# First input projection of a two-layer diffusion backbone: which engine splits the first half's weights, and which weights are split a second time

## The chip, the cores and the metric

One core of one Trainium2 chip runs the whole program. The metric is the device time of one execution in microseconds (us); lower is better. The core has five engines with queues of their own that run in order: PE (matmul; PEld is its weight load), DVE (VectorE), ACT (ScalarE), POOL (GpSimd) and SP, which here only issues DMAs.

## The reference, cut to what matters

The change lies in the input projection of the first layer, `u = h @ w_in`: 2304 tokens (256 of context, 2048 latent) by 2816 columns with an inner size of 1024. Its columns go to the convolution branch (value and gate), to attention (q, k, v) and to the gate path z:

```python
def layer_ab(...):
    shift, scale, gate = adaln(c[:, None, :], w_ada, b_ada)
    h = rms_norm(x, norm_g) * (1 + scale) + shift
    u = h @ w_in
    a_val, a_gate = u[..., :A_WIDTH], u[..., A_WIDTH:AB_Q_OFF]
    q, k, v, z = ...                      # more columns of u
    y_a = conformer_conv(a_val, a_gate, conv_w, conv_b, ln_g, ln_b)   # depthwise, 31 taps
    y_b = blocked_attn(q, ...k, ...v)
    y = jnp.concatenate([y_a, y_b], axis=-1) * jax.nn.silu(z)
    x = x + gate * (y @ w_out)
```

All of it is float32, to float32 accuracy.

## The kernel before, in words

A float32 product is made of three matmuls on rounded halves. Each operand is split: ACT copies it to a rounded type (`hi`), and a second engine makes `lo = src - hi`. PE then adds hi·hi, hi·lo and lo·hi (`mm_channel`, lines 431 to 433, for outputs with channels on the partitions; `mm_token`, lines 440 to 442, for q, k and v). The second engine of the split is an argument: `split` (line 447) uses DVE unless told otherwise, `load_w` (line 399) uses POOL unless told otherwise.

The projection works in **two halves** of three token blocks of 384 (b = 0 to 2, then 3 to 5). In each half it goes through eleven **tasks**, each with its own 256 weight columns: g0, u0, g1, u1 (gate and value of the convolution), kv, q0, q1 and z0 to z3. A task of kind g, u or z makes six products of 24 matmuls; a task of kind kv or q makes nine, each followed by a chain of small steps in `qk`: ACT squares, DVE sums, POOL takes the power -0.5 (line 750), DVE scales (line 751), POOL multiplies by the rope tables (lines 755 and 759), DVE adds and splits (lines 763, 767, 770), PE transposes (line 779).

The weights of one task are two tiles (`kh` = 0, 1) in each of `whi` and `wlo`, whose pool `wp` holds four; so two tasks' weights fit, and a task's weights can be split only after the task before the last has released its tiles. In the first half `load_w` brings raw weights (`wraw`, two buffers) for the next task and splits them; `keep_w` writes the split halves to DRAM (`w_d`), and in the second half `kept_w` reads them back. g0 and u0 of the first half are special: they are loaded and split on DVE ahead of everything (`w_gu`, lines 618 to 645).

Beside this, DVE runs the depthwise convolution of the half as a background: `conv` yields one tap at a time (line 533, one instruction over 1151 or 1168 positions), and `advance` issues a number of taps before each product (3.2 or 3.6 for g, u and z, 1.1 after each q or k product). At the last z task of the first half, `prep_block` normalises, transposes (line 369), modulates (line 372, DVE) and splits (lines 380 and 381) the tokens of the second half.

The order on each engine is set by a scheduler with a timeline of its own, which places instructions by their data's availability on that timeline; taps are kept in program order. So an edit of an engine moves rows all around it.

Of the kernel before, what the change touches and what calls it, by code (L numbers as in the profile page):

```python
# [83 lines left out]
class Build:  # L84
# [365 lines left out]
    def ab_proj(self):  # L450
        nc, I, cp = self.nc, self.I, self.cp
        w = I["ab_w_in"][0]
# [3 lines left out]
        with ExitStack() as es:  # L456
# [4 lines left out]
            rp = self.pool(es, "rp", 2)  # L461
            wp = self.pool(es, "wp", 4)
# [24 lines left out]
            def small():  # L487
                rows = zp.tile([CONV, 512], F32, name="cwrows", tag="tz")
                nc.sync.dma_start(rows[:], I["ab_conv_w"][0])
                for c in range(4):  # L490
                    pt = pt_p.tile([P, 512], F32, name="cwt", tag="ptr")
                    nc.tensor.transpose(pt[:, :CONV], rows[:, c * P : (c + 1) * P], self.ident[:CONV, :CONV])
                    nc.vector.tensor_scalar(out=cw[:, c], in0=pt[:, :CONV], scalar1=0.5, scalar2=None, op0=ALU.mult)
                nc.sync.dma_start(cb[:], I["ab_conv_b"][0].rearrange("(c p) -> p c", p=P))
                for j, (nm, sgn) in enumerate((("ab_q_norm_g", -0.125), ("ab_k_norm_g", 1.0))):
                    g, gs = gain[:, 2 * j], gain[:, 2 * j + 1]
                    nc.sync.dma_start(g, I[nm][0:1, :].broadcast_to((P, 64)))
                    if sgn != 1.0:
                        nc.vector.tensor_scalar(out=g, in0=g, scalar1=sgn, scalar2=None, op0=ALU.mult)
                    nc.vector.tensor_copy(  # L500
                        gs.rearrange("p (i a) -> p i a", a=2), g.rearrange("p (i a) -> p i a", a=2)[:, :, ::-1]
                    )
# [13 lines left out]
            def advance(n):  # L516
                credit[0] = credit[0] + n if taps else 0.0
                while credit[0] >= 1 and taps:
                    f = taps.pop(0)
                    if next(f, None) is not None:  # L520
                        taps.insert(min(1, len(taps)), f)
                        credit[0] -= 1
# [56 lines left out]
            def convolve(j, us, half):  # L579
                for c, u in enumerate(us):  # L580
                    if half == 0:
                        nc.vector.tensor_copy(halo[:, 2 * j + c], u[:, 1151:1182])
                    taps.append(conv(u, 2 * j + c, half))
# [25 lines left out]
            ada, w_gu, hold = [], [], [[], []]  # L609
# [44 lines left out]
            for b in range(3):  # L654
# [8 lines left out]
                for c in range(2):  # L663
                    glu(0, c, b, us[c], sums[1, c, b])
                nxt[b] = hl[b]
            for i in range(2):
                self.keep_w(self.w_d[i], w_gu[i])
            small()
            ea.close()
            q3 = self.pool(er, "q3", 5, side="right")  # L670
            q2 = self.pool(er, "q2", 2, side="right")
            convolve(0, us, 0)
            ws_next = self.load_w(self.raws(rp), wp, w, 768)
            tasks = [("g", 0), ("u", 0), ("g", 1), ("u", 1), ("kv", 0), ("q", 0), ("q", 1), ("z", 0), ("z", 1), ("z", 2), ("z", 3)]
            col = {"g": 512, "u": 0, "kv": 1536, "q": 1024, "z": 1792}
            for half in range(2):
                blocks = range(3 * half, 3 * half + 3)
                for ti, (kind, j) in enumerate(tasks):
                    if half == 0 and ti < 2:
                        continue  # L680
                    ws = ws_next
                    if half == 0:
                        self.keep_w(self.w_d[ti], ws)
                    nk, nj = tasks[(ti + 1) % 11]
                    if half * 11 + ti < 10:
                        ws_next = self.load_w(self.raws(rp), wp, w, col[nk] + 256 * nj)
                    elif half * 11 + ti < 21:
                        ws_next = self.kept_w(wp, self.w_d[(ti + 1) % 11])
                    if kind in "guz":
                        for f in late:  # L690
                            next(f, None)
                        late.clear()
                        if half == 1 and (kind, j) == ("z", 0):
                            er.close()
                            self.load_kv()
                        if kind == "u":
                            us = pads(half, j)
                        order = [(c, b) for c in range(2) for b in blocks]
                        last = half == 0 and ti == len(tasks) - 1
                        if last or ti == 0:  # L700
                            order = [(c, b) for b in blocks for c in range(2)]
                        if half == 0 and 2 <= ti < 4:
                            for i in range(9):
                                rope(9 * ti - 18 + i)
                        for c, b in order:
                            advance(PZ[half] if kind == "z" else PG[half])
                            ps = mm_tile()
                            self.mm_channel(ps[:, :384], ws, nxt[b], c, slice(0, 384))
                            if kind == "g":
                                gate(j, c, b, ps)  # L710
                            elif kind == "u":
                                glu(j, c, b, us[c], ps)
                            else:
                                t = zp.tile([P, 384], F32, name="tz", tag="tz")
                                nc.scalar.activation(t[:], ps[:, :384], AF.Silu)
                                nc.scalar.dma_start(self.gz_d[2 * j + c, :, b * 384 : b * 384 + 384], t[:])
                            if last and c == 1:
                                prep_block(b + 3)
                        if kind == "u":
                            convolve(j, us, half)  # L720
                        continue
                    nh = 2 if kind == "kv" else 4
                    for b in blocks:
                        for i in range(3):
                            tt = 3 * b + i
                            ps = mm_tile()
                            self.mm_token(ps[:, :256], ws, nxt[b], slice(i * P, (i + 1) * P))
                            late.append(self.qk(qp, q2, q3, sp, pt_p, rope_d, ps, tt, kind, j, nh))
                            next(late[-1])
                            if len(late) > 3:  # L730
                                next(late.pop(0), None)
                            advance(PQ[half])
                for b in blocks:
                    del nxt[b]
# [1161 lines left out]
```

## Time and profile before

| what | us |
|---|---|
| median of 3 runs | 2914.79 |
| lowest, highest of them | 2907.32, 2920.73 |
| the profiled execution | 2907.36 |
| its span | 2905.6 |
| mean granted TensorE clock, share of full | 0.977 |

The profile is of one execution. Times in it run from its span's start; the projection takes about the first 685 us, and the first layer's attention follows. The rows on which the next section draws are shown ahead of it. Busy time is not time on the path: PE is busy almost everywhere, so what counts is where it stands idle or runs at the lower clock, and what ended that.

### The profile page before, as it was taken

The numbers are of one execution on the slowest core, as the hardware profiler recorded it, in microseconds if no ns is written. First come the engines' busy times: TensorE is split into PE (matmuls) and PEld (weight loads), VectorE is DVE, ScalarE is ACT, GpSimd is POOL, SyncE is SP. The second block draws the span as 40 slices with busy tenths as digits, with TensorE's granted clock in tenths as the row PEclk, the third lists the DMA queues.
The fourth block names the chain that finished last, engine by engine and source line by source line (L and its number), as shares of the span: only waits on it lengthen the run. The fifth ranks groups of instructions, "written<-read, shape, count | busy, mean of one in ns | idle before, by whom it ended". The sixth has DMA issues, their size and how long they took to land.

```text
span 2905.6 us, 40946 instructions
## 1 busy us (share of the span) xinstructions
PE 2752.1 (95%) x14481; PEld 2118.0 (73%) x14481; DVE 1825.2 (63%) x2867; ACT 1116.8 (38%) x2081; POOL 1416.4 (49%) x1151
## 2 busy tenths in 40 slices
PE   7998799999999999999999999999999997889898
PEld 5988799996444444444447788988898876788787
DVE  4798868898777878878977454101212246777563
ACT  3223120312445555555553223123222236677321
POOL 2568610711666787887885652222222214445342
PEclk9999899998999999999999999999999998999999
DMA  9546332474533433321216543333434269998862
GB/s 297 192 131 207 129 123 97 135 239 151 149 107 103 144 98 106 120 68 44 73 33 210 192 159 143 138 112 112 143 132 136 82 197 230 235 230 196 270 210 80
DMA packets 346808, 432.27 MB, mean 149 GB/s; under 512 B 55900, under 2 KB 260236, under 8 KB 341611
## 3 DMA queue, kind: packets, MB, share of 16 engines
q1 hardware_dynamic: 310891, 403.03, 46.2%
q10 hardware_dynamic: 35712, 26.62, 2.9%
q8 instruction: 114, 1.87, 0.3%
q14 instruction: 91, 0.75, 0.1%
HBM read 281.87 MB, written 152.84 MB: 150 GB/s over the span
## 4 chain that ended last, share of the span: by engine, by line
PE 62%; DMA 10%; DVE 3%; POOL 2%; issue 2%; ACT 1%; SPq 0%; POOLq 0%; ACTq 0%; DVEq 0%
PE av L922 9%; PE s L907 8%; PE mm L431 6%; PE mm L433 6%; PE mm L432 6%; PE m L884 6%; PE mo L1107 4%; PE mo L1108 4%; PE mo L1109 4%; DMA nv<-v_d 3%; DMA nk<-k 3%; PE mm L442 1%; PE mm L441 1%; PE mm L440 1%; DMA pat<-pat_d 1%
## 5 line engine op out<-in xcount | busy, mean ns | idle before, releaser
L886 DVE TENSOR_REDUCE ast<-m 128x1 f32<-128x512 f32 (+1 forms) x656 | 397.9, 626 | 145.9 <-PE m L884 143.8
L912 ACT ACTIVATE pr<-s 128x512 f32<-128x512 f32 x584 | 343.2, 595 | 311.7 <-PE s L907 269.6
L947 POOL TENSOR_TENSOR accp<-accp,pr 128x512 f32<-128x512 f32 x283 | 400.1, 1414 | 86.0 <-ACT pr L912 71.3
L447 POOL TENSOR_TENSOR wlo<-wraw,whi 128x1024 fp32r<-128x1024 f32 x64 | 202.4, 3169 | 380.3 <-ACT whi L446 380.2
L533 DVE SCALAR_TENSOR_TENSOR acc<-u,cw,acc 128x1151 f32<-128x1151 f32 (+1 forms) x240 | 353.0, 1526 | 0.0
L922 PE MATMUL av<-pr,vt 128*64 128x512 f32 x1168 | 315.7, 619 | 0.0
L433 PE MATMUL mm<-hi_ab,wlo 128*128 128x384 f32 x768 | 258.7, 338 | 16.8 <-POOL wlo L447 15.5
L432 PE MATMUL mm<-lo_ab,whi 128*128 128x384 f32 x768 | 259.8, 339 | 0.0
L431 PE MATMUL mm<-hi_ab,whi 128*128 128x384 f32 x768 | 256.2, 340 | 3.3 <-ACT hi_ab L380 1.9
L431 PE MATMUL mm<-hi_cd,whi 128*128 128x512 f32 x640 | 250.8, 392 | 1.1 <-ACT hi_cd L380 1.1
L432 PE MATMUL mm<-lo_cd,whi 128*128 128x512 f32 x640 | 250.1, 391 | 0.4 <-DVE lo_cd L381 0.4
L433 PE MATMUL mm<-hi_cd,wlo 128*128 128x512 f32 x640 | 246.7, 390 | 0.0
L947 DVE TENSOR_TENSOR accd<-accd,pr 128x512 f32<-128x512 f32 x165 | 169.2, 1026 | 1.3 <-DVE accd L947 0.5
L1664 DVE TENSOR_TENSOR nlo<-npt,nhi 128x512 fp32r<-128x512 f32 x192 | 123.6, 645 | 69.3 <-ACT nhi L1662 68.5
L884 PEld LDWEIGHTS m<-k1h,q 128*128 128x128 f32 x328 | 61.8, 188 | 133.8 <-DVE ast L886 79.8
L433 PEld LDWEIGHTS mm<-hi_ab,wlo 128*128 128x128 f32 x768 | 145.5, 190 | 17.8 <-POOL wlo L447 15.8
L884 PEld LDWEIGHTS m<-k0h,q 128*128 128x128 f32 x328 | 63.5, 196 | 125.2 <-DVE ast L886 82.1
L1626 POOL TENSOR_SCALAR npr<-npr,nst 128x640 f32<-128x640 f32 (+1 forms) x128 | 108.0, 857 | 89.5 <-DVE nst L1625 64.1
L372 DVE TENSOR_SCALAR ht<-ptr,scale,shift 128x384 f32<-128x384 f32 (+2 forms) x96 | 61.2, 671 | 141.1 <-PE ptr L369 140.5
L431 PEld LDWEIGHTS mm<-hi_ab,whi 128*128 128x128 f32 x768 | 144.9, 190 | 5.3 <-ACT hi_ab L380 2.9
L432 PEld LDWEIGHTS mm<-lo_ab,whi 128*128 128x128 f32 x768 | 145.4, 189 | 0.9 <-issue 0.8
L431 PEld LDWEIGHTS mm<-hi_cd,whi 128*128 128x128 f32 x640 | 120.4, 188 | 26.1 <-ACT hi_cd L380 1.6
(321 smaller groups left out, 6931.4 us busy)
## 6 DMA issues: line engine op xcount, KB each, us to landing
wraw<-in_cd_w_in_dram SPq DMA_DIRECT2D x46, 512.0 KB, 3.8
pat_d<-big SPq DMA_DIRECT2D x72, 256.0 KB, 4.0
nk<-k SPq DMA_DIRECT2D x32, 576.0 KB, 12.7
pat<-pat_d SPq DMA_DIRECT2D x24, 768.0 KB, 6.0
nv<-v_d SPq DMA_DIRECT2D x128, 128.0 KB, 7.3
adaraw<-in_ab_w_ada_dram SPq DMA_DIRECT2D x24, 512.0 KB, 8.2
adaraw<-in_cd_w_ada_dram SPq DMA_DIRECT2D x24, 512.0 KB, 3.7
w_d<-whi SPq DMA_DIRECT2D x22, 512.0 KB, 2.8
```

Of the source, the lines that this page charges most:

```text
L431: nc.tensor.matmul(ps, a, hh[:, k, cols], start=k == 0, stop=False)
L432: nc.tensor.matmul(ps, a, hl[:, k, cols], start=False, stop=False)
L433: nc.tensor.matmul(ps, b, hh[:, k, cols], start=False, stop=k == KT - 1)
L447: (eng or nc.vector).tensor_tensor(out=lo, in0=src, in1=hi.bitcast(F32), op=ALU.subtract)
L533: ins = nc.vector.scalar_tensor_tensor(out=acc[:, :n], in0=u[:, tap : tap + n], scalar=cw[:, ch, tap : tap + 1], in1=acc[:, :n], op0=ALU.m ...
L884: nc.tensor.matmul(ps[:, :n], lhs, kt[hp // 2][0][:, a : a + n], start=True, stop=True)
L886: nc.vector.tensor_reduce(out=s["st"][:, qt, col : col + 1], in_=ps[:, :n], axis=AX.X, op=ALU.min)
L907: nc.tensor.matmul(ps[:], kt[hp // 2][key][:, k * P : k * P + P], s[x][:].rearrange("p j n -> p (j n)"), start=key == 0, stop=key == 1,)
L912: nc.scalar.activation(pr[:], ps[:], AF.Exp, scale=-1.0)
L922: nc.tensor.matmul(s["av"][x * 64 : x * 64 + 64], vt[:, k - 1 + x, kv * 64 : kv * 64 + 64], s["pr"][k - 1 + x][:], start=k == 1, stop=k == ...
L947: eng.tensor_tensor(out=s[name][:], in0=first_in[:], in1=s["pr"][k][:], op=ALU.add)
L1664: return lambda: nc.vector.tensor_tensor(out=lo[:, :o], in0=pt[:, :o], in1=hi[:, :o].bitcast(F32), op=ALU.subtract)
```

## The change

The first-half weights from g1 to z3 (nine tasks, 18 splits) are split by DVE in place of POOL. The weights of g0 and u0 are no longer written to DRAM; when the second half needs them they are loaded raw and split once more, by DVE (4 splits). The reads of kept weights remain for the other nine tasks of the second half.

```diff
@@ ab_proj
                 nxt[b] = hl[b]
-            for i in range(2):
-                self.keep_w(self.w_d[i], w_gu[i])
             small()
...
             convolve(0, us, 0)
-            ws_next = self.load_w(self.raws(rp), wp, w, 768)
+            ws_next = self.load_w(self.raws(rp), wp, w, 768, eng=nc.vector)
...
-                    if half * 11 + ti < 10:
-                        ws_next = self.load_w(self.raws(rp), wp, w, col[nk] + 256 * nj)
+                    if half * 11 + ti < 12:
+                        ws_next = self.load_w(self.raws(rp), wp, w, col[nk] + 256 * nj, eng=nc.vector)
                     elif half * 11 + ti < 21:
-                        ws_next = self.kept_w(wp, self.w_d[(ti + 1) % 11])
+                        ws_next = self.kept_w(wp, self.w_d[ti + 1])
```

In the order that the scheduler makes, three places matter. Line numbers of the changed kernel behind its line 665 are two lower than before: its line 761 is 763 before, 765 is 767.

**DVE in the z tasks, before.** From the last step of the last q product (`hl`) to the first block of the second half; `acc` are convolution taps, `ht` is line 372, `lo_ab` line 381.

```order
L763 TENSOR_TENSOR t_3055<-t_3055,qsq 128x256
L767 TENSOR_TENSOR hl<-t_3055,hl 128x4x64
L533 SCALAR_TENSOR_TENSOR acc<-u,cw,acc 128x1151 x47
L372 TENSOR_SCALAR ht<-ptr,scale_234,shift_233 128x384 x2
L533 SCALAR_TENSOR_TENSOR acc<-u,cw,acc 128x1151
L372 TENSOR_SCALAR ht<-ptr,scale_234,shift_233 128x384
```

The same place in the changed kernel; the three pairs of `wlo` are the splits for z2, for z3 and for the second g0.

```order
L765 TENSOR_TENSOR hl<-t_3047,hl 128x4x64
L533 SCALAR_TENSOR_TENSOR acc<-u,cw,acc 128x1151 x2
L336 TENSOR_SCALAR st<-st 128x1
L533 SCALAR_TENSOR_TENSOR acc<-u,cw,acc 128x1151 x6
L447 TENSOR_TENSOR wlo<-wraw,whi 128x1024
L533 SCALAR_TENSOR_TENSOR acc<-u,cw,acc 128x1151 x2
L447 TENSOR_TENSOR wlo<-wraw,whi 128x1024
L533 SCALAR_TENSOR_TENSOR acc<-u,cw,acc 128x1151 x12
L447 TENSOR_TENSOR wlo<-wraw,whi 128x1024
L533 SCALAR_TENSOR_TENSOR acc<-u,cw,acc 128x1151
L447 TENSOR_TENSOR wlo<-wraw,whi 128x1024
L533 SCALAR_TENSOR_TENSOR acc<-u,cw,acc 128x1151 x15
```

After these stand the pair for g0 with one tap between, four taps, and then the first `ht`. So 47 taps have become 43 taps and six splits.

**DVE at the end of the first second-half block, before.** These are the last rows of block 3 and the first `u` of the second half.

```order
L372 TENSOR_SCALAR ht<-ptr,scale_234,shift_233 128x384 x2
L533 SCALAR_TENSOR_TENSOR acc<-u,cw,acc 128x1151 x2
L381 TENSOR_TENSOR lo_ab_3812<-ht,hi_ab_3811 128x384 x2
L564 COPY u<-halo 128x31
L336 TENSOR_SCALAR st<-st 128x1
L575 SCALAR_TENSOR_TENSOR u<-tg,mm 128x384
```

The same rows in the changed kernel.

```order
L372 TENSOR_SCALAR ht<-ptr,scale_234,shift_233 128x384 x2
L447 TENSOR_TENSOR wlo<-wraw,whi 128x1024
L533 SCALAR_TENSOR_TENSOR acc<-u,cw,acc 128x1151
L447 TENSOR_TENSOR wlo<-wraw,whi 128x1024
L533 SCALAR_TENSOR_TENSOR acc<-u,cw,acc 128x1151
L381 TENSOR_TENSOR lo_ab_3808<-ht,hi_ab_3807 128x384 x2
L533 SCALAR_TENSOR_TENSOR acc<-u,cw,acc 128x1151 x4
```

The pair of splits for the second u0 now stands ahead of the last two `lo_ab` of block 3. Its `whi` copies stand likewise on ACT, and they write tiles that z3 uses to its end.

**POOL among the last q products and in the z tasks, before.** `qst` is line 750, `t` and `qsq` are lines 755 and 759.

```order
L755 TENSOR_TENSOR t_2946<-qraw,tab 128x256
L759 TENSOR_TENSOR qsq<-qraw,tab 128x256
L755 TENSOR_TENSOR t_3000<-qraw,tab 128x256
L759 TENSOR_TENSOR qsq<-qraw,tab 128x256
L750 TENSOR_TENSOR qst<-qst,mhalf 128x4
L340 TENSOR_SCALAR xt<-xt,st 128x1024
L339 TENSOR_TENSOR st<-st,mhalf 128x1
L340 TENSOR_SCALAR xt<-xt,st 128x1024
L755 TENSOR_TENSOR t_3055<-qraw,tab 128x256
L759 TENSOR_TENSOR qsq<-qraw,tab 128x256
L447 TENSOR_TENSOR wlo<-wraw,whi 128x1024 x4
```

The same place in the changed kernel.

```order
L753 TENSOR_TENSOR t_2992<-qraw,tab 128x256
L757 TENSOR_TENSOR qsq<-qraw,tab 128x256
L753 TENSOR_TENSOR t_3047<-qraw,tab 128x256
L757 TENSOR_TENSOR qsq<-qraw,tab 128x256
L339 TENSOR_TENSOR st<-st,mhalf 128x1
L340 TENSOR_SCALAR xt<-xt,st 128x1024
L565 MEMSET u 128x15
```

POOL has no split left; under the z tasks it holds only the scaling of one token tile (lines 339 and 340), which belongs to block 4.

## Rows read from the trace of the kernel before

**Rows 1.** The view of windows, one for each stretch of the projection: kv, q0 and q1 of the first half; the same of the second half; z0 to z2; the wait ahead of z3; z3; second g0. Columns: stretch, its length, then PE, PEld, DVE, ACT and POOL busy us (instructions), granted clock, DMA share, GB/s.

```profile
152.10:258.00 105.90, 92.47 (x717) 90.69 (x717) 94.82 (x154) 31.93 (x83) 77.59 (x74) 0.92 0.47 150
490.60:579.20 88.60, 85.36 (x715) 84.08 (x713) 73.87 (x139) 25.64 (x74) 61.08 (x67) 1.00 0.43 137
258.00:336.60 78.60, 77.49 (x457) 76.75 (x457) 73.57 (x66) 23.04 (x42) 55.21 (x23) 1.00 0.56 190
336.60:352.60 16.00, 0.49 (x3) 0.17 (x1) 13.76 (x11) 0.49 (x1) 16.00 (x2) 0.60 0.03 12
352.60:382.20 29.60, 29.59 (x169) 29.41 (x170) 19.08 (x23) 5.28 (x11) 2.29 (x1) 0.93 0.47 165
382.20:415.70 33.50, 31.24 (x192) 29.60 (x191) 21.11 (x43) 15.23 (x30) 8.23 (x12) 1.00 0.37 145
```

**Rows 2.** The view of waits, PE, 0 to 700 us. Columns: us in total, times, longest.

```profile
PE mm L433 <- POOL wlo L447: 15.5, 1, 15.5
```

**Rows 3.** The instructions on the tile `wlo`, 0 to 700 us: count, shortest/median/longest in ns, first and last start in us.

```profile
L447 POOL TENSOR_TENSOR wlo<-wraw,whi x18: 2370/2918/41862, 93.1 to 352.5; 128x1024 fp32r<-128x1024 f32 x18
L447 DVE TENSOR_TENSOR wlo<-wraw,whi x2: 1217/1222/1226, 22.2 to 24.8; 128x1024 fp32r<-128x1024 f32 x2
```

**Rows 4.** The timeline of POOL, 286 to 360 us: start, length, what, count, idle time before it and what ended that.

```profile
288.26 2.93 POOL L447 TENSOR_TENSOR wlo<-wraw,whi 128x1024 fp32r<-128x1024 f32 x1 [7.10 <-ACT whi L446]
292.68 3.31 POOL L447 TENSOR_TENSOR wlo<-wraw,whi 128x1024 fp32r<-128x1024 f32 x1 [1.49 <-ACT whi L446]
310.70 44.20 POOL L447 TENSOR_TENSOR wlo<-wraw,whi 128x1024 fp32r<-128x1024 f32 x2 [14.70 <-ACT whi L446]
```

**Rows 5.** The timeline of DVE, 283 to 400 us.

```profile
283.54 66.82 DVE L533 SCALAR_TENSOR_TENSOR acc<-u,cw,acc 128x1151 f32<-128x1151 f32 x47
363.12 1.26 DVE L372 TENSOR_SCALAR ht<-ptr,scale,shift 128x384 f32<-128x384 f32 x2 [12.76 <-PE ptr L369]
...
383.90 1.02 DVE L381 TENSOR_TENSOR lo_ab<-ht,hi_ab 128x384 fp32r<-128x384 f32 x2
```

**Rows 6.** The timeline of PE around the wait ahead of z3.

```profile
336.75 0.34 PE L432 MATMUL mm<-lo_ab,whi 128*128 128x384 f32 x1
352.61 0.69 PE L433 MATMUL mm<-hi_ab,wlo 128*128 128x384 f32 x1 [15.53 <-POOL wlo L447]
```

**Rows 7.** The view of windows right behind that wait, columns as in Rows 1.

```profile
352.60:356.70 4.10, 4.09 (x13) 4.09 (x14) 0.00 (x0) 0.00 (x0) 2.29 (x1) 0.50 0.56 221
356.80:361.00 4.20, 4.20 (x26) 4.20 (x25) 0.00 (x0) 0.49 (x1) 0.00 (x0) 1.00 0.88 298
```

**Rows 8.** The timeline of ACT in z2: the evictions of its last two products.

```profile
332.61 0.49 ACT L715 ACTIVATE tz<-mm 128x384 f32<-128x384 f32 x1 [3.67 <-PE mm L433]
...
336.77 0.49 ACT L715 ACTIVATE tz<-mm 128x384 f32<-128x384 f32 x1 [3.67 <-PE mm L433]
```

**Rows 9.** The view of groups by line, DVE, of four stretches in this order: 104 to 283 us, 300 to 351, 490.6 to 579.2 and 600 to 680. Columns: count, busy us, mean ns of one, idle time before.

```profile
L533 DVE SCALAR_TENSOR_TENSOR acc<-u,cw,acc 128x1151 f32<-128x1151 f32 x63 | 102.6, 1663 | 0.0
...
L533 DVE SCALAR_TENSOR_TENSOR acc<-u,cw,acc 128x1151 f32<-128x1151 f32 x38 | 50.6, 1417 | 0.0
...
L533 DVE SCALAR_TENSOR_TENSOR acc<-u,cw,acc 128x1168 f32<-128x1168 f32 x26 | 41.1, 1592 | 0.0
...
L533 DVE SCALAR_TENSOR_TENSOR acc<-u,cw,acc 128x1168 f32<-128x1168 f32 x58 | 78.3, 1429 | 0.0
```

**Rows 10.** The timelines of DVE and POOL, 125 to 134 us.

```profile
124.78 9.68 DVE L533 SCALAR_TENSOR_TENSOR acc<-u,cw,acc 128x1151 f32<-128x1151 f32 x4
...
126.27 6.98 POOL L447 TENSOR_TENSOR wlo<-wraw,whi 128x1024 fp32r<-128x1024 f32 x2 [6.61 <-ACT whi L446]
```

**Rows 11.** The view of waits, PE: first four rows kv to q1 of the first half (152.1 to 258 us), last two the same of the second half (490.6 to 579.2).

```profile
PE ptr L779 <- ACT hl L769: 5.0, 1, 5.0
PE ptr L779 <- DVE hl L767: 3.9, 3, 1.6
PE mm L440 <- DVE qraw L751: 3.1, 3, 1.5
PE mm L440 <- DVE u L575: 1.3, 1, 1.3
...
PE mm L440 <- DVE qraw L751: 2.9, 4, 0.8
PE ptr L779 <- DVE hl L767: 0.3, 1, 0.3
```

**Rows 12.** The view of windows, stretches of lower clock between kv and q1, columns as in Rows 1.

```profile
172.40:179.30 6.90, 6.51 (x31) 6.51 (x32) 6.40 (x14) 2.19 (x8) 4.74 (x6) 0.51 0.30 86
227.00:230.50 3.50, 2.90 (x13) 2.90 (x14) 3.38 (x3) 1.20 (x3) 3.50 (x3) 0.51 1.00 350
240.60:247.50 6.90, 4.99 (x24) 4.83 (x25) 5.73 (x12) 2.55 (x6) 4.31 (x6) 0.51 0.37 105
```

**Rows 13.** Groups by line, ACT, 85 to 420 us, and the page, part 6 (DMA issues: count, KB each, median us to landing).

```profile
L446 ACT ACTIVATE whi<-wraw 128x1024 fp32r<-128x1024 f32 x18 | 19.1, 1060 | 33.4 <-PE mm L432 29.6 <-DMA wraw<-in_ab_w_in_dram 2.4 <-PE mm L433 1.5
...
wraw<-in_cd_w_in_dram SPq DMA_DIRECT2D x46, 512.0 KB, 3.8
...
w_d<-whi SPq DMA_DIRECT2D x22, 512.0 KB, 2.8
```

## The prediction

> **What bounds the kernel now.** I read the windows of the projection first. PE is busy nearly all of each stretch but one: ahead of z3 there are 16.0 us with three PE instructions [rows 1]. The view of waits names one wait of 15.5 us, PE's first matmul with `wlo` of z3 on POOL's split [rows 2], and PE's timeline shows the same 15.53 us between 336.75 and 352.61 [rows 6]. The reader is to see next what that split is: POOL's 18 weight splits of the first half take 2.37 us at least and 2.92 in the median, and one takes 41.86 [rows 3]. It starts at 310.70, as soon as its `whi` is there, and its successor ends the pair's 44.20 us [rows 4]. DVE tells the rest: from 283.54 it runs 47 taps without a pause for 66.82 us, to 350.36 [rows 5], and the long split ends some 2 us after, about what a split takes by itself. So POOL stood behind DVE's taps for as long as these came without a gap. The other two splits under this run took 2.93 and 3.31 [rows 4].
>
> The second place is kv to q1: 105.9 us in the first half and 88.6 in the second for the same matmuls, at a mean granted clock of 0.92 against 1.00 [rows 1]. There PE waits 5.0 + 3.9 + 3.1 + 1.3 = 13.3 us for the chain of small steps and a late eviction, against 3.2 us in the second half [rows 11], and 17.3 us run at half clock, the level of 1.2 GHz, with 14.4 us of PE work [rows 12].
>
> **Part 1: the long split goes.** In the changed order z3's splits stand on DVE, behind 22 taps and two other splits from the end of the last q product. A tap without POOL beside it takes 50.6 / 38 = 1.33 us of DVE's time [rows 9], a DVE split 1.22 [rows 3]. With the 47-tap run's start at 283.54 as the anchor, z3's first split starts at about 283.5 + 22 × 1.33 + 2 × 1.22 = 315 and the second ends near 319. Its `whi` needs the end of z1, near 312, so DVE does not wait there either. PE asks for it at 336.75 [rows 6]: 18 us of slack. The 15.5 us go. Behind the wait PE runs 13 matmuls in 4.1 us at 0.50 and then 26 in 4.2 at 1.00 [rows 7], so the lower clock that follows costs 4.1 / 2 = 2.05 us, and goes too. Together **-17.6 us**.
>
> What is late next is block 3's preparation, which DVE does behind its taps. Before, DVE had finished the run at 350.36 and then sat idle 12.76 us for PE [rows 5]. Without the wait, PE reaches z3 at 336.75, needs 8.3 us for two products (4.16 each, the distance of two evictions [rows 8]), transposes three column groups, and after 33 further matmuls (33 / 24 × 4.16 = 5.7 us) wants their buffers back: about 352. DVE gets to the first `ht` after 43 taps and six splits, 283.5 + 43 × 1.33 + 6 × 1.22 = 348. So this holds with 4 us to spare if DVE reaches the anchor no later than now.
>
> **Part 2: does DVE reach the anchor as early?** Up to the first `ht`, 20 splits of 1.22 us are new on DVE. The two of g1 fall where DVE has little to do, ahead of the taps; 18 remain, 22.0 us. But POOL's splits were not free to DVE. Four taps with two POOL splits beside them took 9.68 us [rows 10], where 4 × 1.33 = 5.3: 2.2 us for each split, nearly twice what DVE needs to do it itself. Likewise the 47 taps: 66.82 - 62.5 = 4.3 us for the two splits under them [rows 5]. From 104 to 283 us 63 taps took 102.6 where 83.8 were enough [rows 9]: 18.8 us too many. Part of this is POOL's work for q, which stays: in the second half, without splits, 26 taps between kv and q1 took 41.1 where, at 78.3 / 58 = 1.35, 35.1 were enough [rows 9], so 6.0. The relief is 18.8 - 6.0 + 4.3 = 17.1, at the most 16 × 2.2 = 35 and at the least the 8.7 us of the four splits seen singly. I take 17.1, since it rests on 63 taps. Net, DVE's load grows by 5 us (13 at the most, -13 at the least) over 180 us in which it is nearly full, and loses four taps (5.3 us) ahead of the first `ht`: **0 on the path**, with 4 us of slack.
>
> By a rule of the Trainium skill (the page SBUF — State Buffer, section "Who interferes with whom") the port that VectorE and GpSimd share is held for one whole instruction by whoever starts first, also against a VectorE instruction with two SBUF inputs; taken by itself it would let a split wait one tap, as 2.93 and 3.31 us do, and not some thirty, as 41.86 does. It would make the long split an accident with another cause.
>
> **Part 3: kv to q1.** Six splits leave POOL and six come to DVE. The ends are 0 and the full distance to the second half, 105.9 - 88.6 = 17.3. Each first wait of 5.0 and 1.3 us stands at the start of kv, where DVE is behind with taps; there the relief is larger than the added splits, two POOL splits costing 4.4 and two DVE splits 2.4. The later waits, 7 us, hang on DVE's chain, which gets no lighter. I take the first kind, less what DVE cannot make up: **-5 us**.
>
> **Part 4: second u0.** DVE's pair of splits for u0 stands ahead of the last two `lo` of block 3, and needs the tiles that z3 frees at its end. With z3 from 336.75 and 29.6 - 2.05 us long [rows 1, 7], it ends near 364.3. DVE, from 348, has eight `ht`, eight `lo` (1.26 and 1.02 us a pair [rows 5]) and ten taps before the last `lo` of block 3: 5.0 + 4.1 + 13.3, and the pair of splits 2.4, which gives 373. The second g0 needs that `lo` 18 matmuls after z3's end, 3.1 us, at 367.4. ACT's copies, 1.06 us each [rows 13], are ready by 366 and are no bound. New wait: 3 to 6 us, less what DVE gains in part 3, and up to half of a stretch like 172.4 to 179.3 at half clock [rows 12], 3.3 us. Between 0 and 9, I take **+5 us**.
>
> **Part 5: queues.** SP issues eight writes less near the start and, for g0 and u0, four raw loads in place of eight reads (3.8 and 2.8 us to landing [rows 13]); no PE wait on these reads is among those that end now, so 0. ACT has four more copies, 4.2 us, in stretches where it is busy less than a third [rows 1]: 0. Behind block 3 the order is that of before and nothing else moves.
>
> **Sum.** -17.6 - 5 + 5 = -17.6 us on the profiled execution, 2907.4 to 2889.8. That execution lies at the bottom of the four known (2907.3, 2907.4, 2914.8, 2920.7, middle 2911.1). From the middle the sum gives 2893.5; I write **2894 us**.
>
> **The rivals.** *The stall is handed on to DVE.* If the relief of part 2 is at its lower end, DVE's load grows by 13 us, the first `ht` comes near 361 and PE, at 352, waits 9 us, with 2 to 3 us of half clock behind it; the last `lo` moves back as much, so part 4 costs 9, and part 3 gives nothing: -17.6 + 11.5 + 9 = +3, 2914. For it: DVE runs 66.82 us without a gap [rows 5], and from kv to q1 is busy 94.8 of 105.9 us [rows 1]. Against it: 2.2 us for each POOL split under taps [rows 10].
>
> *The long split is an accident.* One of 18 is long [rows 3]; if most executions do not have it, part 1 falls away: -5 + 5, 2911. This is also what the rule of the Trainium skill cited in part 2 (SBUF — State Buffer, "Who interferes with whom") gives. Against it: a run without the stall would be some 17 us shorter, and of the three timed ones none is below the profiled.
>
> *Slower: DVE's queue stops at splits whose tiles PE has not yet freed.* The pairs for q1, z0, z1, g0 and u0 each need the end of a task on PE, and PSUM evictions for PE stand behind them on DVE. It decides once DVE comes to them ahead of PE by more than PE's free PSUM tiles cover. The nearest price is the longest wait of PE for that chain, 5.0 us, with 3.3 of half clock behind it [rows 11, 12]; five times 8.3 is 41.5, against 17.6 gained: +24, 2935. Against it: DVE is the one that is behind in most of the half.
>
> **Chances.** Forecast 0.58, handed on 0.22, accident 0.12, slower 0.08. About 0.5% (14.6 us) is what a measurement of this kernel can tell from no change. The forecast's gain, 17.6 with terms that can each be off by 5, exceeds that in nine of ten of its cases: faster 0.52; same takes the rest of it and the next two rivals, 0.40; slower 0.08. The range runs from the forecast with 12 us more in part 3, or with no wait in part 4, 2878, to the handed-on stall, 2914.
>
> **What would show it.** In the profile after: no POOL work on `wlo`, no PE wait ahead of z3, z3 starting its first 48 matmuls right behind z2 (part 1); taps of 1.33 us in the z tasks and fewer long ones before (part 2); kv to q1 nearer 100 than 106 us (part 3); a PE wait for `lo` of block 3 in the second g0, a few us long (part 4). I am wrong if PE waits in z3 for `ht` by more than 5 us, if a POOL step of the q chain is starved under taps, or if the first half's tasks from g1 to z2 get longer.

## The result, and the profile after

| | median us | lowest, highest | executions | ratio to before, 95% interval |
|---|---|---|---|---|
| before | 2916.62 | 2907.32, 2920.73 | 4 | |
| changed | 2892.37 | 2889.40, 2895.14 | 4 | 0.993 [0.9904, 0.9955] |
| changed, in a later series (before there: 2910.20, 25 executions) | 2890.28 | 2881.68, 2906.29 | 8 | 0.9936 [0.9913, 0.996] |

The kernel is faster by 0.7%, some 20 us; 2894 was forecast. The profiled execution took 2895.14 us, its span is 2893.3 at a mean granted clock of 0.978. In the changed kernel a line behind 665 has a number two lower than before.

The windows of the same stages as in [rows 1]: kv to q1, z0 to z2, z3, second g0; columns as there.

```profile
154.20:252.30 98.10, 89.05 (x715) 87.84 (x713) 86.08 (x154) 31.06 (x81) 64.67 (x68) 0.95 0.50 159
252.40:329.80 77.40, 77.35 (x457) 77.14 (x457) 72.65 (x73) 25.23 (x44) 20.83 (x18) 1.00 0.65 222
329.80:357.70 27.90, 27.90 (x172) 27.77 (x172) 27.90 (x31) 7.90 (x14) 0.00 (x0) 1.00 0.32 105
357.70:396.70 39.00, 33.16 (x189) 31.55 (x188) 30.74 (x50) 16.28 (x31) 7.37 (x12) 0.91 0.21 72
```

z3 with the wait ahead of it took 16.0 + 29.6 = 45.6 us; it takes 27.9, all of it PE work. kv to q1 is 7.8 us shorter: PE's idle time there goes from 105.90 - 92.47 = 13.4 to 9.0 us, and its busy time falls by 3.4 us as the granted clock rises from 0.92 to 0.95. The second g0 is 5.5 us longer. From the view of waits, PE, 0 to 700 us, the row `PE mm L433 <- POOL wlo L447` of [rows 2] is gone. Of 154.2 to 252.3 us, kv to q1, these three rows are all that it has, in place of the four of [rows 11].

```profile
PE mm L440 <- DVE qraw L749: 4.0, 3, 2.4
PE mm L440 <- ACT vv L771: 2.9, 2, 2.4
PE ptr L777 <- DVE hl L765: 2.1, 2, 1.6
```

The splits, all on DVE (as [rows 3]):

```profile
L447 DVE TENSOR_TENSOR wlo<-wraw,whi x24: 1206/1216/1758, 21.9 to 360.6; 128x1024 fp32r<-128x1024 f32 x24
```

The group of the taps from 104 to 283 us (as the first of [rows 9]):

```profile
L533 DVE SCALAR_TENSOR_TENSOR acc<-u,cw,acc 128x1151 f32<-128x1151 f32 x69 | 98.5, 1456 | 0.0
```

The timeline of DVE from the last split for the second g0 to the last taps of the first half (as [rows 5]):

```profile
333.57 1.22 DVE L447 TENSOR_TENSOR wlo<-wraw,whi 128x1024 fp32r<-128x1024 f32 x1
334.71 5.40 DVE L533 SCALAR_TENSOR_TENSOR acc<-u,cw,acc 128x1151 f32<-128x1151 f32 x4
340.02 1.85 DVE L372 TENSOR_SCALAR ht<-ptr,scale,shift 128x384 f32<-128x384 f32 x3
...
363.08 1.01 DVE L381 TENSOR_TENSOR lo_ab<-ht,hi_ab 128x384 fp32r<-128x384 f32 x2
364.02 5.39 DVE L533 SCALAR_TENSOR_TENSOR acc<-u,cw,acc 128x1151 f32<-128x1151 f32 x4
```

No split takes over 1.8 us, 69 taps now fit into 98.5 us where 63 took 102.6, and DVE is at the first `ht` at 340.0, ten us behind z3's start at 329.8, early enough that PE does not wait there.

**The new gap in the second g0.** It does not hang on block 3's `lo`, which DVE has done at 364.1. Its chain, followed from PE backwards, begins with PE's timeline:

```profile
371.37 0.34 PE L433 MATMUL mm<-hi_ab,wlo 128*128 128x384 f32 x1
376.58 0.90 PE L369 MATMUL ptr<-ident,xt 128*128 128x128 f32 x3 [4.88 <-POOL xt L340]
```

POOL's, with the tile that PE waited for:

```profile
374.75 0.56 POOL L339 TENSOR_TENSOR st<-st,mhalf 128x1 f32<-128x1 f32 x1 [5.17 <-DVE st L336]
375.41 1.12 POOL L340 TENSOR_SCALAR xt<-xt,st 128x1024 f32<-128x1024 f32 x1
```

DVE's step ahead of it, which waited for ACT's sum of squares:

```profile
374.51 0.15 DVE L336 TENSOR_SCALAR st<-st 128x1 f32<-128x1 f32 x1 [2.14 <-ACT jk L335]
```

SP's, with the load of that tile:

```profile
368.96 0.44 SPq L325 DMA_DIRECT2D xt<-in_x_dram  x1
```

And the window right behind the gap, columns as above:

```profile
376.60:381.80 5.20, 4.85 (x18) 4.16 (x19) 4.85 (x9) 3.18 (x8) 4.99 (x6) 0.50 0.01 3
```

PE stands still for 4.88 us and then runs 5.2 us at 0.50, the level of 1.2 GHz. It waits for POOL's normalised token tile, the third of block 4; that waits for the sum of squares, and that for the load issued at 368.96. The tile is taken from the pool `up`, which also holds the convolution's input `u`, and the load is issued while DVE ends the last four taps (364.02 to 369.41), which free their `u` tiles. In SP's queue it stands right behind two writes of `acc`, which wait for the same taps. In the kernel before, this load went out 3.4 us behind z3's end and PE waited 1.0 us for the tile; here it went out 11.3 us behind.

From the first matmul to the end of the projection the terms are: start of kv +2.1, kv to q1 -7.8, z0 to z2 -1.2, z3 -17.7, second g0 +5.5, the rest +1.8 us; its last matmul ends at 667.4 in place of 684.7 us, 17.3 earlier. The whole profiled execution is only 12.2 us shorter; experiment 5 says why.

### The profile page after: what moved, and what is told of

It is laid out like the page before. It is cut to its first block, busy times and chain, and to the rows that moved or that the text cites. A ratio compares the mean times of both kernels' runs of the same rounds, so it can differ in the third digit from the quotient of the medians.

```text
span 2893.3 us, 40920 instructions
## 1 busy us (share of the span) xinstructions
PE 2755.2 (95%) x14481; PEld 2118.0 (73%) x14481; DVE 1821.2 (63%) x2889; ACT 1120.5 (39%) x2085; POOL 1329.2 (46%) x1133
## 4 chain that ended last, share of the span: by engine, by line
PE 61%; DMA 11%; DVE 3%; POOL 2%; issue 2%; ACT 1%; SPq 0%; POOLq 0%; ACTq 0%; DVEq 0%
PE av L920 8%; PE s L905 8%; PE mm L433 6%; PE mm L432 6%; PE mm L431 6%; PE m L882 6%; PE mo L1105 4%; PE mo L1106 4%; PE mo L1107 4%; DMA nv<-v_d 4%; DMA nk<-k 3%; PE mm L440 1%; PE mm L441 1%; PE mm L442 1%; PE npt L1655 1%
## 5 line engine op out<-in xcount | busy, mean ns | idle before, releaser
L533 DVE SCALAR_TENSOR_TENSOR acc<-u,cw,acc 128x1151 f32<-128x1151 f32 (+1 forms) x240 | 337.0, 1454 | 0.0
L447 POOL TENSOR_TENSOR wlo<-wraw,whi 128x1024 fp32r<-128x1024 f32 x46 | 111.5, 2428 | 326.8 <-ACT whi L446 326.6
L433 PE MATMUL mm<-hi_ab,wlo 128*128 128x384 f32 x768 | 257.9, 337 | 1.5 <-DMA wlo<-w_d 1.5
L433 PE MATMUL mm<-hi_cd,wlo 128*128 128x512 f32 x640 | 246.7, 390 | 0.0
L433 PEld LDWEIGHTS mm<-hi_ab,wlo 128*128 128x128 f32 x768 | 145.0, 189 | 2.4 <-DMA wlo<-w_d 2.2
L882 PE MATMUL m<-k0h,q 128*128 128x512 f32 (+1 forms) x328 | 134.5, 438 | 5.9 <-DVE ast L884 5.8
```

The costliest lines, as they stand in the source:

```text
L433: nc.tensor.matmul(ps, b, hh[:, k, cols], start=False, stop=k == KT - 1)
L533: ins = nc.vector.scalar_tensor_tensor(out=acc[:, :n], in0=u[:, tap : tap + n], scalar=cw[:, ch, tap : tap + 1], in1=acc[:, :n], op0=ALU.m ...
L882: nc.tensor.matmul(ps[:, :n], lhs, kt[hp // 2][0][:, a : a + n], start=True, stop=True)
```

## The experiments

The stages of the kernels of experiments 1 to 5, in us, from the profile of each; those of experiment 6 are given there. "End" is the end of the projection's last matmul. The table goes by the matmuls' own times, so it can differ by 0.1 us from a window, whose bounds are rounded.

| kernel | kv to q1 | z3 | second g0 | end | median, ratio to before [95%] |
|---|---|---|---|---|---|
| before | 105.9 | 45.6 | 33.5 | 684.7 | |
| before again | 104.9 | 45.2 | 33.1 | 685.9 | 2914.89 (one) |
| only z3's splits on DVE | 105.7 | 28.0 | 36.8 | 668.6 | 2896.14, 0.9955 [0.9936, 0.9974] |
| only g0, u0 split twice | 107.8 | 37.1 | 42.7 | 690.3 | 2918.70, 1.002 [1.0003, 1.0037] |
| all first-half splits on DVE, g0, u0 kept | 97.1 | 27.9 | 36.9 | 661.4 | 2887.27, 0.9928 [0.9903, 0.9953] |
| changed | 98.1 | 27.9 | 39.0 | 667.4 | 2892.37, 0.993 [0.9904, 0.9955] |
| changed again | 98.4 | 27.9 | 38.7 | 663.9 | 2890.28, 0.9936 [0.9913, 0.996] |
| changed, fifth buffer | 98.3 | 27.9 | 31.2 | 659.4 | 2882.08, 0.9907 [0.988, 0.9933] |
| kept, fifth buffer | 99.6 | 28.0 | 30.3 | 659.3 | 2881.64, 0.9891 [0.9865, 0.9918] |

### 1. Is the long split an accident?

The kernel before, without an edit.

> The kernel before, unchanged, profiled once more. Theory (POOL starves behind taps that DVE runs without a gap): the order on the engines is fixed, so the first of z3's two splits is long again, 35 us or more, PE waits 10 to 16 us ahead of z3, and z3 with that wait takes about 45 us. Rival (the long split was an accident of one execution): no split above 10 us, z3 takes 28 to 30 us, and the execution is some 17 us shorter than the first profiled one, near 2890.

Its instructions on `wlo`:

```profile
L447 POOL TENSOR_TENSOR wlo<-wraw,whi x18: 2362/2896/41821, 95.8 to 354.1; 128x1024 fp32r<-128x1024 f32 x18
```

The window of z3 with the wait:

```profile
338.20:383.40 45.20, 29.71 (x172) 29.22 (x171) 32.81 (x34) 5.78 (x12) 18.30 (x2) 0.85 0.33 112
```

41.82 us against 41.86, at the same instruction. The accident falls.

### 2. z3 alone, and the rest of part 1

```diff
-                        ws_next = self.load_w(self.raws(rp), wp, w, col[nk] + 256 * nj)
+                        ws_next = self.load_w(self.raws(rp), wp, w, col[nk] + 256 * nj, eng=nc.vector if ti == 9 else None)
```

> The kernel before with one edit: z3's two splits on DVE, all others left on POOL, g0 and u0 kept in DRAM as before. Theory (the 41.86 us split is the whole gain in the z tasks): the wait ahead of z3 goes and z3 takes 28 us in place of 45.6, so 15 to 18 us less on the attention's start, about 2893 to 2897 in the median if before is at 2911 to 2916; kv to q1 stays at 104 to 107 us. Rival (the gain comes from DVE doing all splits, and the starved split only stood where PE had slack): 0 to 6 us.

Windows of kv to q1, z3 and the second g0:

```profile
152.60:258.30 105.70, 90.95 (x716) 88.95 (x715) 95.95 (x154) 32.83 (x83) 78.42 (x75) 0.94 0.48 153
...
335.80:363.90 28.10, 28.10 (x173) 27.66 (x172) 28.10 (x28) 5.77 (x12) 0.00 (x0) 1.00 0.34 113
363.90:400.60 36.70, 32.11 (x189) 30.44 (x187) 28.23 (x51) 15.34 (x30) 8.24 (x12) 0.95 0.39 146
```

Two splits of 18 take the whole 17.6 us out of z3, leave kv to q1 as it was, and put 3.2 us into the second g0, with a PE wait of 3.1 us for POOL's `xt` again. By the medians it is 15.4 us. The other sixteen splits were moved as well in the next kernel, with `eng=nc.vector` in both calls of `load_w` and nothing else of the diff.

> Part 1 of the change alone: all 18 first-half splits on DVE; the splits of g0 and u0 are kept in DRAM and read back in the second half as before, so DVE has four splits fewer (4.9 us) and ACT four copies fewer at the half's end. Theory A (the 4.88 us gap of PE in the second g0 of the changed kernel hangs on a buffer of the convolution's input that the last taps free, so on when DVE is through with its taps): the taps end 4 to 5 us earlier, the gap shrinks to 0 to 2 us, second g0 takes 34 to 36 us in place of 39.0, and the kernel is 3 to 6 us faster than the changed one. Theory B (the forecast: the pair of splits for u0 ahead of block 3's last low halves makes the wait): the same, but with a PE wait for the low halves gone, which the changed kernel's trace did not have. Rival (the gap has another cause): second g0 stays at 39 us, and the kernel equals the changed one.

kv to q1 falls to 97.1 us: this gain belongs to the sixteen splits that left POOL, as it is missing with z3's pair alone. The second g0 is 36.9 us, 2.1 less than in the changed kernel, its wait for `xt` 2.6 us in place of 4.9. That is the direction of theory A, but less than it wanted (0 to 2 us, 34 to 36). The load of the tile did go out earlier, 6.6 us behind z3's end in place of 11.3, but it was 5.9 us and not 4.4 until ACT could begin on the tile; why, no run shows. Whether the kernel as a whole is faster than the changed one stays open: the two ratios differ by less than their intervals.

### 3. g0 and u0 split twice, alone

```diff
-            for i in range(2):
-                self.keep_w(self.w_d[i], w_gu[i])
...
-                    if half * 11 + ti < 10:
-                        ws_next = self.load_w(self.raws(rp), wp, w, col[nk] + 256 * nj)
+                    if half * 11 + ti < 12:
+                        ws_next = self.load_w(self.raws(rp), wp, w, col[nk] + 256 * nj, eng=nc.vector if half * 11 + ti >= 10 else None)
...
-                        ws_next = self.kept_w(wp, self.w_d[(ti + 1) % 11])
+                        ws_next = self.kept_w(wp, self.w_d[ti + 1])
```

> Part 2 of the diff alone: the first half's 18 splits stay on POOL, g0 and u0 are not kept and are loaded and split again, on DVE, for the second half. Theory (the splits done twice are no gain by themselves; DVE owes PE more at the half's end): the long POOL split and PE's wait ahead of z3 stay, second g0 takes 34 to 39 us in place of 33.5, and the kernel equals the one before or is up to 6 us slower. Rival (the gain came with the writes and reads that fall away): 5 us or more faster than before.

By the ratio it is slower by 0.2%, as the theory has it. The first three of five rows of the view of waits, PE, 300 to 425 us:

```profile
PE mm L433 <- POOL wlo L447: 5.9, 1, 5.9
PE mm L432 <- DVE lo_ab L381: 3.1, 2, 2.9
PE ptr L369 <- POOL xt L340: 2.6, 1, 2.6
```

Here the wait for block 3's `lo` that the prediction looked for appears: DVE has them done at 388.0, 10.5 us behind z3's end at 377.5, and PE stands 2.9 us. In the changed kernel DVE had them 6.4 us behind z3's end, and PE did not wait. The second g0 takes 42.7 us, 9.2 more than before: the upper end that the prediction gave this term, and above the 34 to 39 us expected here. The wait ahead of z3 was 5.9 and not 15 us; the long split is there (32.27 us), but it began later, at 314.5, in a shorter run of taps. And a second one appeared (below).

### 4. The fifth buffer

```diff
-            up = self.pool(es, "up", 4)
+            up = self.pool(es, "up", 5)
```

> The changed kernel with a fifth buffer in the pool of the convolution's input, from which the raw token tiles of the second half's blocks are taken too. Theory A (the gap in the second g0 comes from the load of block 4's third token tile, which waits for the last first-half taps to free its buffer): that load is issued before the taps end, PE's 4.88 us gap and the half clock behind it go, second g0 takes 33 to 34 us in place of 39.0, the kernel is 4 to 6 us faster than the changed one, near 2887. Rival (DVE is behind as such, so the next thing that it owes PE comes as late): second g0 takes 37 us or more, with PE waiting for another DVE step.

The window of the second g0:

```profile
360.40:391.70 31.30, 30.59 (x192) 29.72 (x191) 30.16 (x50) 14.30 (x29) 11.45 (x10) 1.00 0.19 74
```

SP's timeline, the load of block 4's third token tile and those of block 5's three:

```profile
266.63 0.34 SPq L325 DMA_DIRECT2D xt<-in_x_dram  x1
...
357.13 1.29 SPq L325 DMA_DIRECT2D xt<-in_x_dram  x3
```

PE's timeline, the first transposes of block 4, here and, in the second row, in the changed kernel:

```profile
357.34 0.49 PE L369 MATMUL ptr<-ident,xt 128*128 128x128 f32 x3
...
354.66 0.38 PE L369 MATMUL ptr<-ident,xt 128*128 128x128 f32 x2
```

The view of waits, PE, 329 to 397 us, has one row:

```profile
PE mm L432 <- DVE lo_ab L381: 0.7, 1, 0.7
```

One tile more is loaded early, at 60.86 us, so block 4's third one goes out at 266.6 in place of 369.0 us, long before the last taps. (Block 5's three go out at 357.13, in the changed kernel at 354.46.) PE's transposes show the same: here they take three tiles of block 4 at a time from the start, where the changed kernel had only two and came to the third at 376.58. The gap and the half clock go, and the second g0 is 7.7 us shorter than in the changed kernel, where 5 to 6 were expected. So the gap hung on the buffer. (The load now also stands ahead of the writes of `acc` in SP's queue; no run separates the two.) In the medians the kernel is 8 us faster than the changed one; the intervals of the two ratios overlap, and it is the stage of the trace that tells them apart. The same with g0 and u0 kept and read back:

> Both earlier edits together: all first-half splits on DVE, g0 and u0 kept in DRAM and read back, and a fifth buffer in the pool of the convolution's input. Theory (two separate costs of the changed kernel at the end of the first half: the load that waits for a buffer, 4.88 us of gap with half clock behind it, and the four splits done twice, some 4.9 us of DVE): PE has no gap above 1 us in the second g0, which takes 31 to 32 us, and the second z tasks take 103 us; the projection ends at 657 to 660 us and the kernel is at 2878 to 2884. Rival (with the buffer there, the splits done twice cost nothing, as DVE is ahead again): the same as the changed kernel with the fifth buffer alone, within 2 us at the projection's end.

PE has no wait at all in z3 and the second g0, but the projection ends at 659.3 against 659.4 us: the rival was right. With the buffer there, splitting g0 and u0 twice costs nothing and brings nothing, as far as one profile of each shows. Both kernels are the best of this study, 0.9% to 1.1% below before.

### 5. What differs from execution to execution

> The changed kernel, unchanged, on the same chip as the others. Theory: the projection ends at 667 us within 2 us, second g0 takes 39 us with the gap of 4 to 5 us, and what differs from execution to execution lies in the first layer's attention, which takes 1061 to 1073 us. Rival (the 5 to 6 us that seemed to be lost again in the attention of the changed kernel belong to the change): its attention takes 1067 to 1069 us again, where that of the kernel before takes 1062.

The window of the first layer's attention, from the projection's end on. Before:

```profile
684.70:1746.50 1061.80, 1037.55 (x4370) 566.22 (x4368) 806.28 (x1213) 502.34 (x887) 743.70 (x574) 0.99 0.39 118
```

Before again:

```profile
685.90:1758.00 1072.10, 1047.81 (x4368) 570.62 (x4367) 799.31 (x1213) 502.48 (x887) 740.12 (x574) 0.98 0.39 117
```

Changed:

```profile
667.40:1735.30 1067.90, 1040.70 (x4368) 565.93 (x4368) 806.58 (x1213) 502.33 (x887) 743.09 (x574) 0.99 0.39 118
```

Changed again:

```profile
663.90:1728.90 1065.00, 1041.00 (x4368) 568.35 (x4367) 801.55 (x1213) 502.15 (x887) 742.63 (x574) 0.99 0.39 118
```

The changed kernel's projection ended at 663.9 us the second time, 3 us from the expected 667, which is outside the 2 us allowed; its second g0 took 38.7 us with a gap of 5.2. Its attention took 1065.0 us, so the rival's 1067 to 1069 did not come back. The kernel before takes 1061.8 and 1072.1 us in a stage that the change does not touch, the second time with as many instructions and 10 us more PE busy time. The 17.3 us that the projection gains are reduced to 12.2 in the two profiled executions as that of before had the shortest attention of the four; that the change gives anything back there, these four executions do not show.

### 6. What lets POOL in

The prediction said that POOL stands behind DVE as long as taps come without a gap. But two splits under the same run got in at the next tap [rows 4]. Counting the taps that DVE had run one right behind the other when the split was issued (since any other DVE instruction, or since POOL was last in, the tap in progress with them), the profiles of before and before again show: with 4 or 5 taps it was in at the next one, four times of four; with 11 it was shut out to the run's end, twice of two. So breaks were put into the run: a memset of 128x1 on DVE behind taps of the first half.

```diff
+            brk = op1.tile([P, 1], F32, name="brk")
...
+                    if half == 0 and tap % 4 == 0:
+                        self.tc.keep_in_program_order(nc.vector.memset(brk[:], 0.0))
```

> The kernel before, with a memset of 128x1 on DVE behind every fourth tap index of the first half (28 of them); the splits stay on POOL. Theory (POOL is shut out because the two-input taps follow each other without a gap): at the next memset POOL gets in, no split takes above 8 us, PE's wait ahead of z3 goes, and the kernel is at 2892 to 2898. Rival (the long split has another cause, in POOL or in that split's data): it stays at 35 us or more, and the kernel at 2905 to 2920.

No split takes over 3.62 us and PE's wait for `wlo` is gone; the projection ends at 671.5 us, the median is 2898.36, the ratio 0.9959 [0.9944, 0.9975]. DVE's last memset ahead of z3's splits and the taps after it, then POOL's two splits:

```profile
306.07 0.06 DVE L540 MEMSET brk<- 128x1 f32 x1
307.37 13.69 DVE L534 SCALAR_TENSOR_TENSOR acc<-u,cw,acc 128x1151 f32<-128x1151 f32 x7
...
311.63 6.88 POOL L447 TENSOR_TENSOR wlo<-wraw,whi 128x1024 fp32r<-128x1024 f32 x2 [14.71 <-ACT whi L446]
```

But z3's first split got in at 312.7, at the end of the fourth tap behind a memset, between two taps that follow each other as closely as all others. So the next memset is not what it waited for; what counts is the break that already lay behind it. The seven taps take 13.69 us, where 7 × 1.33 = 9.3: 2.2 us for each split that got in. Two more kernels hold the condition `ch >= 2 and tap == 7`, then `tap == 6`, in its place.

> The kernel before, with a memset of 128x1 on DVE behind tap 7 alone, of the two channels whose taps run in the z tasks. By the traces so far a POOL split got in at the next tap where at most 5 taps had run without a pause, and not before the run's end where 9 or more had. Here z3's first split is issued about 7 taps behind the memset, between the two. Theory (what counts is how long DVE's run already is): it is either in within two taps or out until 350 us, and this places the limit on either side of 7. Rival (the length of the run has nothing to do with it): a length in between, such as 5 to 25 us.

> The same with the memset behind tap 6, so that some 9 taps have run without a pause when z3's first split is issued. Theory: 9 is too many, the split lasts 35 us or more and PE waits 13 to 16 us ahead of z3, as without any memset. Rival (any memset among the taps lets POOL in, or the added instruction shifts the time of issue by luck): the split takes under 5 us and z3 28 us.

The timeline of DVE with the memset behind tap 7:

```profile
304.01 0.06 DVE L540 MEMSET brk<- 128x1 f32 x1
305.32 25.64 DVE L534 SCALAR_TENSOR_TENSOR acc<-u,cw,acc 128x1151 f32<-128x1151 f32 x16
```

That of POOL:

```profile
311.87 5.92 POOL L447 TENSOR_TENSOR wlo<-wraw,whi 128x1024 fp32r<-128x1024 f32 x2 [13.02 <-ACT whi L446]
```

DVE with the memset behind tap 6:

```profile
299.00 0.06 DVE L540 MEMSET brk<- 128x1 f32 x1
300.32 49.23 DVE L534 SCALAR_TENSOR_TENSOR acc<-u,cw,acc 128x1151 f32<-128x1151 f32 x37
```

POOL:

```profile
309.69 44.37 POOL L447 TENSOR_TENSOR wlo<-wraw,whi 128x1024 fp32r<-128x1024 f32 x2 [14.52 <-ACT whi L446]
```

In the first, (311.87 - 305.32) / 1.33 = 4.9, so the split is issued in the fifth tap, and both splits are through in 5.92 us. (The expectation's 7 was two too many, so the limit stays between 5 and 8.) In the second, (309.69 - 300.32) / 1.33 = 7.0, it comes in the eighth, and the first split takes 42.06 us (44.37 with its successor) as without a memset. The projection ends at 673.2 and 683.6 us (before: 684.7 and 685.9); the one execution of each took 2902.33 and 2911.72 us, beside 2911.67 of before. Last, z3's splits in eight pieces:

```diff
+            for k in range(4):
+                (eng or nc.vector).tensor_tensor(out=lo[:, k], in0=src[:, k], in1=hi[:, k].bitcast(F32), op=ALU.subtract)
```

> The kernel before, with z3's two splits on POOL cut into eight instructions of 128x256 in place of two of 128x1024. Theory (once DVE has run some ten two-input taps without a pause, POOL gets no turn until the run ends): the first of the eight is issued after 11 such taps, lasts 35 us or more, the other seven follow behind the run, and PE waits 14 to 18 us ahead of z3. Rival (at each tap's end it is a matter of luck who is next, and one instruction of 18 was unlucky): with eight tries most get in at the next tap, none lasts above 10 us, and PE doesn't wait.

The instructions on `wlo`:

```profile
L449 POOL TENSOR_TENSOR wlo<-wraw,whi x8: 722/729/40589, 311.5 to 356.2; 128x256 fp32r<-128x256 f32 x8
```

The view of waits, PE, 300 to 365 us:

```profile
PE mm L433 <- POOL wlo L449: 14.3, 1, 14.3
```

The first piece, issued in the ninth tap, takes 40.59 us; the others stand behind it in POOL's queue and take 0.73 each once the run is over. So a quarter of the size does not help, and a piece passed over at some 30 tap ends in a row is no lottery at each of them. The one execution took 2915.63 us, beside 2911.67 of before; its projection ends at 684.5.

The kernel of experiment 3 bears this out unasked. The timeline of DVE near 127 us:

```profile
112.93 26.03 DVE L533 SCALAR_TENSOR_TENSOR acc<-u,cw,acc 128x1151 f32<-128x1151 f32 x18
138.88 0.61 DVE L575 SCALAR_TENSOR_TENSOR u<-tg,mm 128x256 f32<-128x256 f32 x2
```

That of POOL:

```profile
127.05 17.64 POOL L447 TENSOR_TENSOR wlo<-wraw,whi 128x1024 fp32r<-128x1024 f32 x2 [11.88 <-ACT whi L446]
```

This split was issued in the ninth undisturbed tap and came in at the first instruction of another kind, `u` with an input in PSUM, after 14.16 us. Over all splits of POOL in the eight profiles where it has any: after 3 to 5 taps, always in at the next (17 times); after 8, 9, 9, 11, 11 and 12 taps, never before the run was broken.

## Why the prediction was right, point by point

**Part 1, -17.6: right to 0.1 us,** and shown by itself in experiment 2 (45.6 to 28.0). Its reason was right in kind and incomplete: gapless taps shut POOL out only once more than five, and at the latest eight, have run. The *accident* had 0.12; before again excludes it. By the rule of the Trainium skill that stood for it (SBUF — State Buffer, "Who interferes with whom") whoever starts first holds the port for its whole instruction; a tap with a POOL split beside it lasts 3.55 us in place of 1.41, which fits it. That a split waits one tap, as the prediction drew from this rule, holds here after three to five taps (17 of 17) and not after eight or more (none of six), and the measurement decides. The same section of the Trainium skill says that a DVE instruction with at most one SBUF input, outside the modes that use both ports, does not contend with GpSimd. At such a one, `u` from PSUM, the split of 14.16 us got in, which agrees.

**Part 2, 0: right.** The relief was put at 17.1 us. By the same working it measures 18.8 - (98.5 - 69 × 1.33) + 4.3 = 16.4, the last term as the z tasks' taps now run at 1.33 us. *Handed on*: not in the changed kernel, where DVE reached the first `ht` at 340.0 and not at 361. But it is what happens where POOL keeps the splits and gets in: with breaks at every fourth tap, or behind tap 7, PE waits 3.9 and 4.2 us for `ht` in z3. This fits the two splits of z3 that got in there, each of which holds up a tap by 2.15 us.

**Part 3, -5: mis-sized, -7.8.** The waits at the start of kv went, as forecast (5.0 + 1.3); the later ones fell only from 7.0 to 6.1 us, and 2.9 us for ACT's `vv` are new, so that PE's idle time went from 13.4 to 9.0. What was left out is the clock: the prediction quoted the stretches at half clock [rows 12] but put nothing for them in this term. With less waiting PE ran less at half clock, and its busy time fell by 3.4 us.

**Part 4, +5: the size right, the mechanism wrong.** The step that failed is "The second g0 needs that `lo` 18 matmuls after z3's end, 3.1 us". PE's timeline in the changed kernel, the first matmul behind z3 and the first that needs one of these last two `lo`:

```profile
357.68 0.33 PE L431 MATMUL mm<-hi_ab,whi 128*128 128x384 f32 x1
...
364.74 0.33 PE L432 MATMUL mm<-lo_ab,whi 128*128 128x384 f32 x1
```

PE runs through most of both products of block 3 first: 38 matmuls and some transposes, 7.1 us, lie ahead of it, and not 18 and 3.1. In experiment 3 it is 38 matmuls and 7.2 us (it stood still until 387.59 for 2.85 us; z3 ended at 377.54). And in the changed kernel the low halves were there 6.4 us behind z3's end, at 364.1, where the forecast had 8.7 (373 against 364.3). So PE did not wait. In their place the next thing that DVE owed PE was late: not a result but a buffer, freed by its last taps, which the prediction had counted as time alone. Experiment 4 shows it; experiment 3 shows that the forecast's wait is there, 2.9 us, when DVE comes later. That 5.5 us came out near +5 is luck.

**Part 5, 0:** nothing seen against it; the reads of kept weights make PE wait 1.5 us in two places of the second half, about as before. The two times to landing that the prediction quoted from [rows 13] belong to other transfers, the second layer's weights and the writes to `w_d`; in the first 700 us of the kernel before, the loads take 6.2 us and the reads 5.2 and 7.3 in the median. The 0 does not hang on them.

***Slower,* 0.08:** did not come. DVE stood at splits for ACT's `whi` six times, 8.2 us, but all six lie before 108 us, ahead of kv; at the pairs that this rival names, for q1, z0, z1, g0 and u0, it did not wait at all.

The sum of -17.6 us lies closer to the projection's own gain, 17.3 us, than its terms deserve, and that too is luck: part 3 gave 2.8 more, and the stages outside the three parts took 2.7 back. The medians fell by 24.3 and 19.9 us. The lower end of the range, 2878, does not follow from its own terms: 12 us more in part 3 give 2882, no wait in part 4 gives 2889, and both together 2877.

## What to carry to other kernels

When one instruction takes ten times as long as its siblings, look at what the engine beside it runs back to back, and for how long it has done so; moving two splits of 18 was worth nearly all of this change. When an engine is behind, list what it frees as well as what it makes: a load that waits for a buffer shows up as a wait for the step after next, under another tile's name. And before a loss late in the span is explained, profile the kernel before the change twice.

## What the runs showed of the hardware

- Two-input DVE instructions of 1.33 us, one right behind the other, kept a POOL instruction out for up to 42.06 us (some 30 tap ends, memset behind tap 6), once 8 or more had run, in six cases of six; after 3 to 5 it was in at the next tap's end, in 17 of 17. The limit between 5 and 8 was not placed, and whether taps, time or something else is counted was not tried.
- A pair of DVE memsets of 59 ns each starts this count anew: with such a pair 4 and 5 taps back, the split was in at the next tap's end though 11 and 9 taps had run since POOL's last turn (experiment 6, every fourth tap and tap 7). The taps around the memsets start only some 10 ns behind their beat of 1.33 us.
- A POOL split that gets in costs DVE 2.15 us (a tap of 3.55 in place of 1.41, in the kernel before at 117.33); the same split takes DVE 1.22 us itself.
